# A two-layer hybrid block on one core: longer latencies in the scheduler's table, and RWKV row sums as single fp32 products

## The chip, the cores and the metric

The kernel runs on one core of a Trainium2 chip. The metric is the device time of one execution in microseconds, measured three times; a separate execution was taken with the hardware profiler, and all rows below come from that one. The engines are called PE (TensorE matmul), PEld (its weight loads), DVE (VectorE), ACT (ScalarE), POOL (GpSimd) and SP (the queue that issues DMAs).

## What is computed

Two layers over a sequence of 1024 tokens of width 1024, all in float32. Each layer normalises and modulates its input, projects it into the inputs of three branches, and adds the gated output projection of the three results. The branches are a chunk-causal latent attention (MLA), a chunked state-space branch (SSD) and an RWKV-7 branch. Cut to what matters here:

```python
h = rms_norm(x, norm_w[l]) * (1.0 + scale) + shift
(q_lat, kv_lat, k_pe, g_mla, z, xbc, dt_raw, r, k, v, w_lo, a_lo, g_rwkv) = split_cols(h @ w_in[l], IN_SPLIT_SIZES)
...
y = jnp.concatenate([y_mla, y_ssd, y_rwkv], axis=-1)
x = x + gate * (y @ w_out[l])
```

The RWKV branch has two sums over the 64 channels of a head, one for the norm of `kk` and one for the bonus term:

```python
kk = kk / jnp.maximum(jnp.sqrt(jnp.sum(kk * kk, axis=-1, keepdims=True)), 1e-12)
...
y = y + jnp.sum(r * k * r_k.astype(f32), axis=-1, keepdims=True) * v
```

## The kernel before

Channels lie on the 128 partitions and tokens along the free axis, in halves of 512 tokens. There are four rounds, one for each layer and half. A round has a dense part (`dense`): the output projection of the round two before it (`outproj`, from the third round on), the norm and modulation (`make_h`, which writes eight pairs of `h` tiles), and the input projection of 37 tiles (`inproj`), whose results go to DRAM. Then come the round's consumers (`consumers`): `rwkv`, which handles two heads at a time in four passes p, then `ssd`, then the attention (`mla_latent`, `mla_proj`, `mla`). The last two output projections end the program.

A large float32 product is computed as three products of rounded parts: each operand is split into a high part (F32R, an ACT copy) and a low part (a DVE subtraction), and high by high, high by low and low by high are summed. `split_w` does this for the weights (tiles `wr`, `wh`, `wl`), `make_h` and `y_split` for the other operand (`h`). The small products are plain fp32; the trace has two PE records for each of these, and one for an F32R product or a transpose.

What each engine does in which order is decided ahead of time by a list scheduler in the kernel itself (class `Plan`). All operations are recorded, and `order` plays them through: each engine takes, among the operations whose inputs it expects to be there, the one of highest rank. RWKV has a slightly higher rank than SSD and attention; the products of the dense part have rank 0 and fill what is left; loads, splits and evacuations rank highest. When an input is there follows from a price for each operation (`cost`, `shape`) and from `LATENCY`, a table of nanoseconds between the end of an operation and the start of one that needs it: the first letter is the engine that made it, the second the engine that waits (S is ScalarE, V VectorE, P TensorE, G GpSimd, D a DMA). The order so found is fixed in the program; on the chip each engine follows it and waits where an input is late. Every operation is issued by one line, L396, so all rows carry that line, and groups are told apart by tile names.

The two row sums are in `rwkv_a1` and `rwkv_a2`. With `PQ` and `PB` at 1 the summed tile (`rt`) is split into `leafh` and `leafl`, two tiles of the pool for attention and SSD, and two F32R products against `bones_r` (a block matrix of ones, rounded once at the start) are added in PSUM. In `rwkv_a1` only 2 columns of that matrix are used, so the result has 2 partitions; in `rwkv_a2` all 128 are used. With `PQ` and `PB` at 0 each is one fp32 product against `bones`. There are 4 passes in 4 rounds, so 16 of each kind. The result of the first is copied by ACT, sent through DRAM (`qd`) and read by `tinv_a`, which starts a chain of 62 small DVE operations; that of the second is multiplied by `v` and kept for the end of the pass. The scheduler's `shape` prices an fp32 product with at most 64 columns of weights at 103 ns, whatever its width, and one with more at 1.73 ns a column.

Of the kernel before, what the change touches and what calls it, by code (L numbers as in the profile page):

```python
# [10 lines left out]
F32R = mybir.dt.float32r  # L11
I32 = mybir.dt.int32
AF = mybir.ActivationFunctionType
# [4 lines left out]
P = 128  # L18
# [37 lines left out]
SG = ()  # L56
# [14 lines left out]
SX, SV, SB = 0, 0, 0  # L71
SG0 = "bbgggggg"
SBP, SBC, SCH = "ra", "ra", 2
SRB = "tf"
PQ = 1
PB = 1
PX = "b2"
WAT = "rv"
LOT = "rl"
# [7 lines left out]

LATENCY = {"SS": 143, "SD": 147, "SV": 142, "SP": 500, "SG": 170, "VS": 128, "VD": 122, "VV": 127, "VP": 500, "VG": 155,  # L90
           "PS": 197, "PV": 196, "PD": 220, "PG": 224, "PP": 3, "GS": 75, "GD": 67, "GV": 60, "GP": 135, "GG": 102,
           "DS": 2200, "DV": 2200, "DP": 2350, "DG": 2200, "DD": 2200}


# [149 lines left out]
class Plan:  # L244
# [41 lines left out]
    def order(self):  # L286
# [12 lines left out]
        def seat(o):  # L299
            t = 0.0  # L300
            for name in o.tiles:
                x = tiles[name]
                if x["free"] is None:
                    tag = x["tag"]
                    n = len(slots[tag]) - (0 if name.startswith("leafl") else owed[tag])
                    if n <= name.startswith("leafh") or not name.startswith("leaf") and name not in line[tag][:n]:
                        parked[tag].append(o)
                        return None
                    t = max([t] + [end + LATENCY[at + o.at] for at, (end, _) in slots[tag][0][1].items()])
                else:  # L310
                    t = max([t] + [end + LATENCY[at + o.at] for at, (end, _) in x["free"].items()])
                if x["bank"]:
                    t = max([t] + [end + LATENCY[at + o.at] for at, (end, _) in x["ends"].items() if at != o.at])
            return t
# [10 lines left out]
        while turn < len(ops):  # L325
# [58 lines left out]
            for j in o.next:  # L384
                ready[j] = max(ready[j], end + LATENCY[o.at + ops[j].at])
                wait[j] -= 1
# [11 lines left out]
def hybrid_layers_kernel(ctx: ExitStack, tc: tile.TileContext, A, out):  # L398
    nc = tc.nc
    plan = Plan(tc)  # L400
    V, S, G, PE, SP = (plan.engine(e, q) for e, q in ((nc.vector, "V"), (nc.scalar, "S"), (nc.gpsimd, "G"),
                                                      (nc.tensor, "P"), (nc.sync, "Q")))
    TQ, AL, AS, BL, BM, BS, EQ = SP, S, S, S, SP, S, SP

    cpool = ctx.enter_context(tc.tile_pool(name="cpool", bufs=1))
# [46 lines left out]
    def s1(n, tag=None, bufs=None):  # L452
        if bufs:
            return sm.tile([P, n], F32, name=nm("s"), tag=tag or f"s{n}", bufs=bufs)
        return sm.tile([P, n], F32, name=nm("s"), tag=tag or f"s{n}")

    def bank(tag):
        return ps.tile([P, HT], F32, name=nm("ps"), tag=tag, bufs=PSB[tag])
# [22 lines left out]
    bones = cst[:, C_BO:C_BO + 128]  # L481
# [17 lines left out]
    for e in range(2):  # L499
        SP.dma_start(cst[64:128, C_MD + 64 * e:C_MD + 64 * e + 64], A["cst"][64:128, C_MD + 64 * (1 - e):C_MD + 64 * (1 - e) + 64])  # L500
    SP.dma_start(mD1[64:128], A["cst"][64:128, C_MD:C_MD + 128])
    bones_r = cpool.tile([P, 128], F32R, name="bones_r")
    S.activation(bones_r, bones, AF.Copy)
    cth = s1(8)
    S.activation(cth, craw, AF.Tanh, scale=0.5)
    V.scalar_tensor_tensor(cth, cth, 1.0, craw, op0=ALU.add, op1=ALU.mult)
# [248 lines left out]
    def rwkv_a1(d, U, p, wa):  # L755
# [32 lines left out]
        pq = bank("ra")  # L788
        if PQ:
            hi, lo = WATS[PX](dt=F32R, leaf="leafh"), WATS[PX](dt=F32R, leaf="leafl")  # L790
# [13 lines left out]
    def rwkv_a2(d, p, u):  # L804
# [29 lines left out]
        pbn = bank("ra")  # L834
        if PB:
            hi, lo = WATS[PX](dt=F32R, leaf="leafh"), WATS[PX](dt=F32R, leaf="leafl")
# [917 lines left out]
```

## Time and profile before

| | |
|---|---|
| median of 3 runs (lowest to highest) | 1953.89 us (1953.27 to 1957.49) |
| the profiled execution | 1953.58 us |
| its span, first to last instruction | 1951.8 us |
| busy in the span: PE, DVE, ACT, POOL | 1825.9, 1619.7, 1205.9, 204.4 us |
| mean granted PE clock | 0.975 |

"Busy" is the time that at least one instruction of the engine ran. The page's second part cuts the span into 40 slices of 48.8 us. A matmul record includes the time until its result has left the array, so the pace of a stream is read from the starts of successive records, not from their lengths.

### The profile page before, as it was taken

The numbers are of one execution on the slowest core, as the hardware profiler recorded it, in microseconds if no ns is written. First come the engines' busy times: TensorE is split into PE (matmuls) and PEld (weight loads), VectorE is DVE, ScalarE is ACT, GpSimd is POOL, SyncE is SP. The second block draws the span as 40 slices with busy tenths as digits, with TensorE's granted clock in tenths as the row PEclk, the third lists the DMA queues.
The fourth block names the chain that finished last, engine by engine and source line by source line (L and its number), as shares of the span: only waits on it lengthen the run. The fifth ranks groups of instructions, "written<-read, shape, count | busy, mean of one in ns | idle before, by whom it ended". The sixth has DMA issues, their size and how long they took to land. (4 is left out here: it accounts for less than half of the span.)

```text
span 1951.8 us, 32300 instructions
## 1 busy us (share of the span) xinstructions
PE 1825.9 (94%) x10220; PEld 1460.7 (75%) x10220; DVE 1619.7 (83%) x4002; ACT 1205.9 (62%) x2520; POOL 204.4 (10%) x302
## 2 busy tenths in 40 slices
PE   5899997999999986989999999998999999999996
PEld 3677775888887764777778778787777877888884
DVE  7898898789897999787788978888788896978774
ACT  5566566676665655566657567675656557675652
POOL 2120011011010101020100001002010020001001
PEclk9999998999999986999999999999999999999997
DMA  7677666765658673744464665854456565753542
GB/s 248 219 201 200 182 198 190 225 200 164 190 152 212 195 205 102 238 132 114 122 165 133 157 203 171 272 170 141 131 146 177 157 203 171 246 162 100 183 144 73
DMA packets 273371, 341.31 MB, mean 175 GB/s; under 512 B 79152, under 2 KB 132016, under 8 KB 273200
## 3 DMA queue, kind: packets, MB, share of 16 engines
q1 hardware_dynamic: 273200, 339.25, 59.6%
q8 instruction: 81, 1.33, 0.3%
q14 instruction: 90, 0.74, 0.1%
HBM read 254.67 MB, written 84.47 MB: 174 GB/s over the span
## 5 line engine op out<-in xcount | busy, mean ns | idle before, releaser
L396 PE MATMUL ps<-h,wh 128*128 128x512 f32 x3136 | 1015.9, 407 | 35.3 <-ACT h L396 21.4
L396 PEld LDWEIGHTS ps<-h,wh 128*128 128x128 f32 x3136 | 581.2, 191 | 166.3 <-ACT h L396 26.8
L396 PE MATMUL ps<-h,wl 128*128 128x512 f32 x1568 | 590.1, 407 | 0.1
L396 PE MATMUL ps<-b,b 128*128 128x512 f32 (+4 forms) x1512 | 384.6, 356 | 10.5 <-DVE b L396 6.3
L396 ACT ACTIVATE wh<-wr 128x512 fp32r<-128x512 f32 (+1 forms) x398 | 246.4, 620 | 211.4 <-PE ps L396 164.3
L396 PEld LDWEIGHTS ps<-h,wl 128*128 128x128 f32 x1568 | 296.8, 191 | 56.7 <-issue 2.5
L396 DVE TENSOR_TENSOR wl<-wr,wh 128x512 fp32r<-128x512 f32 (+1 forms) x398 | 269.7, 680 | 59.4 <-ACT wh L396 41.1
L396 PEld LDWEIGHTS ps<-b,b 128*128 128x128 f32 (+1 forms) x1512 | 232.1, 184 | 67.6 <-DVE b L396 14.5
L396 ACT ACTIVATE b<-b 128x512 f32<-128x512 f32 (+3 forms) x222 | 136.9, 625 | 62.1 <-DVE b L396 25.6
L396 ACT ACTIVATE b<-ps 128x512 f32<-128x512 f32 (+3 forms) x201 | 99.4, 508 | 77.8 <-PE ps L396 73.6
L396 DVE TENSOR_TENSOR b<-b,b 128x512 fp32r<-128x512 f32 (+4 forms) x178 | 121.9, 690 | 18.4 <-ACT b L396 14.5
L396 DVE TENSOR_TENSOR rq<-rq,tmp 128x60 f32<-128x60 f32 (+24 forms) x496 | 109.1, 220 | 6.6
L396 DVE TENSOR_TENSOR tmp<-Q,rq 128x60 f32<-128x60 f32 (+24 forms) x496 | 104.3, 210 | 5.9
L396 ACT ACTIVATE ct<-ps 128x512 f32<-128x512 f32 x150 | 87.8, 588 | 24.1 <-PE ps L396 11.2
L396 PE MATMUL ps<-cst,b 128*128 128x128 f32 x452 | 81.6, 282 | 20.7 <-POOL b L396 15.0
L396 PEld LDWEIGHTS ps<-bx,gg 128*128 128x128 f32 x512 | 76.8, 194 | 32.2 <-DVE bx L396 15.8
L396 POOL COPY halo<-ct 128x3 f32<-128x3 f32 x84 | 28.6, 340 | 621.9 <-ACT ct L396 594.2
L396 PE MATMUL ps<-bx,gg 128*128 128x64 f32 x512 | 80.7, 273 | 9.2 <-DVE bx L396 7.6
L396 PEld LDWEIGHTS ps<-cst,b 128*128 128x128 f32 x452 | 58.4, 146 | 35.1 <-POOL b L396 15.0
L396 POOL TENSOR_TENSOR s<-s,nhalf 128x4 f32<-128x4 f32 (+1 forms) x34 | 54.0, 1591 | 258.1 <-DVE s L396 250.5
L396 DVE SCALAR_TENSOR_TENSOR h<-ps,md,h 128x512 f32<-128x512 f32 x72 | 53.5, 746 | 33.2 <-PE ps L396 32.7
L396 ACT ACTIVATE b<-ps,s,s 128x512 f32<-128x512 f32 (+2 forms) x96 | 63.9, 667 | 27.3 <-DVE s L396 24.3
(196 smaller groups left out, 2612.0 us busy)
## 6 DMA issues: line engine op xcount, KB each, us to landing
wr<-in_w_in_dram SPq DMA_DIRECT2D x282, 256.0 KB
U<-ct SPq DMA_DIRECT2D x84, 257.5 KB
wr<-in_w_out_dram SPq DMA_DIRECT2D x80, 256.0 KB
U<-ct SPq DMA_DIRECT2D x64, 256.0 KB
ct<-in_ada_dram SPq DMA_DIRECT2D x64, 256.0 KB
ri<-U SPq DMA_DIRECT2D x52, 257.5 KB
b<-accd SPq DMA_DIRECT2D x96, 128.0 KB
ct<-yd SPq DMA_DIRECT2D x48, 256.0 KB
```

Of the source, the lines that this page charges most:

```text
L396: o.fn(*o.args, **o.kw)
```

## The change

Two things. First, four entries of the table are raised: ScalarE to VectorE from 142 to 300 ns, VectorE to ScalarE from 128 to 280, TensorE to either from 196 or 197 to 350. The table is used by the scheduler alone; no instruction is altered by it, but their order is. Second, the row sums become single fp32 products, and `bones_r` goes.

```diff
-PQ = 1
-PB = 1
+PQ = 0
+PB = 0
...
-LATENCY = {"SS": 143, "SD": 147, "SV": 142, "SP": 500, "SG": 170, "VS": 128, "VD": 122, "VV": 127, "VP": 500, "VG": 155,
-           "PS": 197, "PV": 196, "PD": 220, ...
+LATENCY = {"SS": 143, "SD": 147, "SV": 300, "SP": 500, "SG": 170, "VS": 280, "VD": 122, "VV": 127, "VP": 500, "VG": 155,
+           "PS": 350, "PV": 350, "PD": 220, ...
...
-    bones_r = cpool.tile([P, 128], F32R, name="bones_r")
-    S.activation(bones_r, bones, AF.Copy)
```

What this does to the order is shown at three places. Tile names carry a number that is shifted between the two programs, so the same tile has two numbers.

**Place A**, PE, where the input projection of the first round ends and that of the second begins. `ps_1246` (before) and `ps_1229` (after) spread the norm of the second half over the partitions; `make_h` needs them, and the products on `h_1247` (before) and `h_1230` (after) need `make_h`. Before:

```order
L396 MATMUL ps_574<-h_261,wh_579 128x512
L396 MATMUL ps_574<-h_260,wl_580 128x512
L396 MATMUL ps_1246<-cst,s_381 128x128 x4
L396 MATMUL ps_1263<-h_1247,wh_1265 128x512
L396 MATMUL ps_1263<-h_1248,wh_1265 128x512
L396 MATMUL ps_1263<-h_1247,wl_1266 128x512
L396 MATMUL ps_1263<-h_1249,wh_1265 128x512
L396 MATMUL ps_1263<-h_1250,wh_1265 128x512
```

After:

```order
L396 MATMUL ps_1229<-cst,s_380 128x128 x4
L396 MATMUL ps_573<-h_235,wh_578 128x512
L396 MATMUL ps_573<-h_234,wl_579 128x512
L396 MATMUL ps_573<-h_247,wh_578 128x512
L396 MATMUL ps_1013<-b_1009,b_953 128x512
L396 MATMUL ps_573<-h_248,wh_578 128x512
L396 MATMUL ps_1013<-b_1010,b_953 128x512
L396 MATMUL ps_1031<-b_1023,b_1020 128x128
L396 MATMUL ps_1013<-b_1009,b_954 128x512
L396 MATMUL ps_1036<-b_1023,b_1020 128x256
L396 MATMUL ps_573<-h_247,wl_579 128x512
L396 MATMUL ps_573<-h_259,wh_578 128x512
```

The products that need `make_h` followed at once; now sixteen others stand between, of the first round's last tile (`ps_573`) and of its attention (`ps_1013`, `ps_1031`, `ps_1036`, `ps_1015`). The three groups of transposes of `mla_latent`, which stood among the `h` products behind this place (`ps_969`, `ps_975`, `ps_976`), stand 227 to 272 PE instructions ahead of it now (`ps_952`, `ps_958`, `ps_959`).

**Place B**, PE, in the output projection that opens the third round. `ps_1817` and `ps_1818` (before), `ps_1788` and `ps_1789` (after) are the steps of the RWKV state chain (`chain`) of the second pass of the second round: each step needs what ACT and DVE made of the one before it. `ps_2022`, `ps_2028` and `ps_2029` belong to `mla_latent` of the same round. Before:

```order
L396 MATMUL ps_1815<-bx_1726,Ez_102 128x128 x4
L396 MATMUL ps_2022<-cst,b_2019 128x128 x4
L396 MATMUL ps_1817<-bx_1787,gg_1725 128x64 x5
L396 MATMUL ps_2028<-cst,b_2026 128x128 x4
L396 MATMUL ps_1817<-bx_1787,gg_1725 128x64 x3
L396 MATMUL ps_2029<-cst,s_2027 128x128 x4
L396 MATMUL ps_1818<-bx_1787,gg_1725 128x64 x2
L396 MATMUL ps_2419<-h_2356,wh_2416 128x512
L396 MATMUL ps_2419<-h_2357,wh_2416 128x512
L396 MATMUL ps_2419<-h_2356,wl_2417 128x512
L396 MATMUL ps_2419<-h_2359,wh_2416 128x512
L396 MATMUL ps_2419<-h_2360,wh_2416 128x512
```

After:

```order
L396 MATMUL ps_2421<-h_2393,wh_2419 128x512
L396 MATMUL ps_1788<-bx_1760,gg_1702 128x64 x2
L396 MATMUL ps_2421<-h_2392,wl_2420 128x512
L396 MATMUL ps_2421<-h_2395,wh_2419 128x512
L396 MATMUL ps_2421<-h_2396,wh_2419 128x512
L396 MATMUL ps_2421<-h_2395,wl_2420 128x512
L396 MATMUL ps_2426<-h_2389,wh_2424 128x512
L396 MATMUL ps_1788<-bx_1760,gg_1702 128x64
L396 MATMUL ps_2421<-h_2398,wh_2419 128x512
L396 MATMUL ps_2426<-h_2390,wh_2424 128x512
L396 MATMUL ps_2421<-h_2399,wh_2419 128x512
L396 MATMUL ps_2426<-h_2389,wl_2425 128x512
```

Before, ten products of the chain and twelve transposes stand with nothing between them; now five to twelve output or attention products stand between every one or two of the chain's, and the transposes of `mla_latent` stand 328 to 375 instructions ahead.

**Place B**, DVE: a piece between two of the weight splits (`wl`) of the same output projection. `tmp` and `rq` are the small operations of `tinv_a`; `b_1975`, `b_1976` and `b_1983` belong to `ssd`. Before:

```order
L396 TENSOR_TENSOR wl_2376<-wr_2374,wh_2375 128x512
L396 TENSOR_TENSOR rq_1741<-rq_1741,tmp_1742 128x10x6
L396 TENSOR_TENSOR b_1975<-b_1973,s_1972 128x512
L396 TENSOR_TENSOR tmp_1742<-Q_1737,rq_1741 128x54
L396 TENSOR_TENSOR b_1976<-b_1974,s_1972 128x512
L396 TENSOR_TENSOR rq_1741<-rq_1741,tmp_1742 128x9x6
L396 TENSOR_TENSOR b_1983<-Sg_117,cd_1924 128x256
L396 TENSOR_TENSOR tmp_1742<-Q_1737,rq_1741 128x48
L396 SCALAR_TENSOR_TENSOR ac_1547<-ct_1607,cact,ac_1547 128x512
L396 TENSOR_TENSOR wl_2383<-wr_2381,wh_2382 128x512
```

After, up to the next split:

```order
L396 TENSOR_TENSOR wl_2343<-wr_2341,wh_2342 128x512
L396 TENSOR_TENSOR rq_1716<-rq_1716,tmp_1717 128x18x4
L396 TENSOR_SCALAR bx_1699<-ps_1728,s_1652 64x64
L396 TENSOR_TENSOR tmp_1717<-Q_1712,rq_1716 128x68
L396 SCALAR_TENSOR_TENSOR b_1992<-b_1992,pp_110,ps_1996 128x512
L396 TENSOR_TENSOR rq_1716<-rq_1716,tmp_1717 128x17x4
L396 TENSOR_TENSOR tmp_1717<-Q_1712,rq_1716 128x64
L396 SCALAR_TENSOR_TENSOR gg_1763<-rt_1741,dp_111,rt_1748 64x8x64
L396 TENSOR_TENSOR rq_1716<-rq_1716,tmp_1717 128x16x4
L396 TENSOR_TENSOR gg_1763<-rt_1739,rt_1748 64x8x64
L396 TENSOR_TENSOR tmp_1717<-Q_1712,rq_1716 128x75
L396 TENSOR_REDUCE s_1729<-bm_1726 128x8
```

The work of `ssd` has left the piece. From the split of the first output weight tile of this round to that of the eleventh (`wl_2369` to `wl_2448` before, `wl_2336` to `wl_2415` after) DVE has 179 instructions before and 118 after; 29 of `ssd`, 13 of the rope table and 9 of the norm and gate of `ssd` have left it. In the stretch of ten input weight tiles ahead of it there were 92 and are 102; in the two stretches behind it (to `wl_2510` and `wl_2577` before, `wl_2477` and `wl_2544` after) there were 139 and 177 and are 135 and 217.

## Rows read from the trace of the kernel before

**Rows 1.** The page: the span, part 1 (busy time, share of the span, instructions of each engine), and of part 2 the busy tenths of PE and the granted clock in tenths, in 40 slices.

```profile
span 1951.8 us, 32300 instructions
...
PE 1825.9 (94%) x10220; PEld 1460.7 (75%) x10220; DVE 1619.7 (83%) x4002; ACT 1205.9 (62%) x2520; POOL 204.4 (10%) x302
...
PE   5899997999999986989999999998999999999996
...
PEclk9999998999999986999999999999999999999997
```

**Rows 2.** Busy time by stretch: from and to in us, length, then busy us and instructions of PE, PEld, DVE, ACT, POOL, the granted clock, the DMA share and GB/s.

```profile
570.00:675.00 105.00, 103.14 (x607) 83.32 (x607) 90.26 (x239) 66.71 (x147) 7.48 (x13) 0.98 0.74 192
...
725.00:775.00 50.00, 30.33 (x119) 21.28 (x117) 45.61 (x119) 29.03 (x51) 6.44 (x5) 0.72 0.36 112
...
675.00:800.00 125.00, 92.19 (x489) 69.31 (x488) 114.52 (x270) 71.88 (x136) 10.74 (x11) 0.84 0.56 165
...
300.00:325.00 25.00, 15.45 (x61) 11.22 (x60) 23.77 (x53) 15.26 (x25) 1.22 (x2) 0.85 0.63 201
325.00:345.00 20.00, 18.74 (x82) 14.80 (x81) 16.12 (x31) 10.64 (x18) 5.17 (x7) 0.94 0.64 175
...
884.00:1340.00 456.00, 450.81 (x2589) 363.11 (x2588) 374.81 (x947) 296.79 (x631) 36.55 (x61) 1.00 0.57 166
```

**Rows 3.** PE's timeline at place A: start, length, what ran, and in brackets how long PE was idle before it and what ended that.

```profile
308.26 0.60 PE L396 MATMUL ps<-cst,s 128*128 128x128 f32 x4
312.28 0.50 PE L396 MATMUL ps<-h,wh 128*128 128x512 f32 x1 [3.42 <-ACT h L396]
...
318.80 0.50 PE L396 MATMUL ps<-h,wh 128*128 128x512 f32 x1 [1.02 <-DVE h L396]
...
323.30 1.11 PE L396 MATMUL ps<-cst,b 128*128 128x128 f32 x4 [3.31 <-DVE b L396]
...
332.00 0.65 PE L396 MATMUL ps<-cst,s 128*128 128x128 f32 x4 [0.80 <-POOL s L396]
```

**Rows 4.** PE's timeline at place B; `ps<-bx,gg` are the steps of the chain, two records each.

```profile
735.12 0.66 PE L396 MATMUL ps<-bx,gg 128*128 128x64 f32 x4
...
738.78 1.12 PE L396 MATMUL ps<-bx,gg 128*128 128x64 f32 x4 [2.16 <-DVE bx L396]
740.14 1.08 PE L396 MATMUL ps<-cst,b 128*128 128x128 f32 x4 [0.25 <-DVE rq L396]
...
743.84 0.69 PE L396 MATMUL ps<-bx,gg 128*128 128x64 f32 x2 [1.82 <-DVE bx L396]
747.20 1.12 PE L396 MATMUL ps<-cst,s 128*128 128x128 f32 x4 [2.67 <-POOL s L396]
```

**Rows 5.** Groups of instructions by form: count, busy us, mean ns of one, then idle time of the engine before them.

```profile
L396 DVE TENSOR_TENSOR leafl<-rt,leafh 128x512 fp32r<-128x512 f32 x32 | 22.0, 687 | 2.5 <-ACT leafh L396 2.1
...
L396 ACT ACTIVATE leafh<-rt 128x512 fp32r<-128x512 f32 x32 | 20.0, 626 | 3.0 <-DVE rt L396 2.6
```

**Rows 6.** Timeline of the first row sum with its split, all engines (the product with 2 columns of weights, amid dense products).

```profile
109.76 0.63 ACT L396 ACTIVATE leafh<-rt 128x512 fp32r<-128x512 f32 x1
...
110.62 0.39 PE L396 MATMUL ps<-leafh,bones_r 128*2 128x512 f32 x1
...
110.63 0.68 DVE L396 TENSOR_TENSOR leafl<-rt,leafh 128x512 fp32r<-128x512 f32 x1
110.85 0.62 PE L396 MATMUL ps<-h,wh 128*128 128x512 f32 x2
...
111.77 0.40 PE L396 MATMUL ps<-leafl,bones_r 128*2 128x512 f32 x1
...
112.01 0.63 PE L396 MATMUL ps<-h,wh 128*128 128x512 f32 x2
```

**Rows 7.** PE's timeline in the attention of the last round: each `ps<-b,b` row of two records is one fp32 product 256 wide.

```profile
1905.34 0.59 PE L396 MATMUL ps<-b,b 128*128 128x256 f32 x2
1905.77 0.27 PE L396 MATMUL ps<-cst,b 128*128 128x128 f32 x1
1905.88 0.60 PE L396 MATMUL ps<-b,b 128*128 128x256 f32 x2
1906.31 0.49 PE L396 MATMUL ps<-cst,b 128*128 128x128 f32 x3
```

**Rows 8.** Groups of DVE instructions between 675 and 800 us, columns as in Rows 5.

```profile
L396 DVE TENSOR_TENSOR b<-b,b 128x512 f32<-128x512 f32 (+3 forms) x24 | 16.4, 683 | 1.5 <-ACT b L396 1.4
L396 DVE TENSOR_TENSOR rq<-rq,tmp 128x48 f32<-128x48 f32 (+24 forms) x39 | 8.6, 220 | 0.1
...
L396 DVE SCALAR_TENSOR_TENSOR b<-b,b 128x512 f32<-128x512 f32 x12 | 7.9, 683 | 0.0
```

More of the change, by code (lines that the diff above doesn't have):

```diff
@@ L86 @@
 HALO = set(range(T_WA, T_G)) | set(range(T_XBC, T_XBC + 8))
-LATENCY = {"SS": 143, "SD": 147, "SV": 142, "SP": 500, "SG": 170, "VS": 128, "VD": 122, "VV": 127, "VP": 500, "VG": 155,
-           "PS": 197, "PV": 196, "PD": 220, "PG": 224, "PP": 3, "GS": 75, "GD": 67, "GV": 60, "GP": 135, "GG": 102,
+LATENCY = {"SS": 143, "SD": 147, "SV": 300, "SP": 500, "SG": 170, "VS": 280, "VD": 122, "VV": 127, "VP": 500, "VG": 155,
+           "PS": 350, "PV": 350, "PD": 220, "PG": 224, "PP": 3, "GS": 75, "GD": 67, "GV": 60, "GP": 135, "GG": 102,
            "DS": 2200, "DV": 2200, "DP": 2350, "DG": 2200, "DD": 2200}
```

## The prediction

> **What bounds the kernel now.** I read the page's first two parts, then the busy time by stretch, then PE's timeline where PE is idle. PE is busy 94% of the span and DVE 83% [rows 1]. Over most of it PE sets the pace: from 884 to 1340 us it is busy 450.81 of 456 us, while DVE has 18% to spare [rows 2]. An instruction more on PE there is paid in full, one less on DVE or ACT gives nothing. PE loses time at a few places: the start, the end, and two in between, where the slices of PE and of its granted clock dip together [rows 1]. Place A is 300 to 345 us, where the second round's `make_h` begins. PE is busy 15.45 of 25 and 18.74 of 20 us there, so it idles 10.8 us, at granted clocks of 0.85 and 0.94 [rows 2]. The waits are for ACT or DVE to finish `h`, and for the transposes of `mla_latent`, with nothing else queued ahead of them [rows 3]. Place B is 675 to 800 us. PE is busy 92.19 of 125 us at a mean clock of 0.84, and in its middle 30.33 of 50 at 0.72 (a mixture of the two levels, 1.0 for 2.4 GHz and 0.5 for 1.2 GHz, after PE has begun to idle); DVE is busy 114.52 of 125, that is 92% [rows 2]. PE's waits there are short chain products, each waiting for the DVE work that follows the one before it, back to back [rows 4]. So at B DVE is the bound, and PE waits in order behind it.
>
> The profiled execution took 1953.58 us, of which 1951.8 are the span; the median of the three runs is 1953.89, or 0.3 above. I sum from 1953.6.
>
> **The change, part by part.** *The row sums.* Gone are 32 ACT copies of 626 ns and 32 DVE subtractions of 687 ns, 20.0 and 22.0 us in all [rows 5]. On PE each pair of F32R products becomes one fp32 product. The pair's pace: from the first product to its follower 0.23 us (110.62 to 110.85), from the second to its follower 0.24 (111.77 to 112.01), together 0.47 [rows 6]. No fp32 product 512 wide stands in the trace. The nearest is 256 wide: 0.43 us from its start to that of the transpose behind it, twice over (1905.34 to 1905.77, 1905.88 to 1906.31) [rows 7], hence 0.86 us for 512 columns. The product with 2 columns of weights streams the same 512 columns, and its F32R form takes no less than the full one's 0.23, so I price both alike. That is 0.39 us more for each, 32 x 0.39 = **+12.5 us** on PE. The bounds are 0, if one fp32 product took no longer than the pair, and +12.5; only the 256-wide row is an fp32 product, so I take the upper end. Amid dense products nothing does; at place B, where PE waits for DVE, a few of the 32 cost nothing. The removed copies and subtractions lie beside PE work except at B, and count there. On each sum's own path the copy and the subtraction vanish and 0.4 us comes in: the first sum's result reaches `qd` about 1 us earlier, which no row shows PE waiting for. `bones_r` was one copy at the start, nothing on the path.
>
> The Trainium skill (TensorE: Matmul & The Clock Gate, section Back-to-back issue gap) says that a sustained stream of products 512 wide runs at about 131 ns for each. By that the removed pair would be 0.26 us, and the change would add an estimated 0.60 a time, 19 us in all instead of 12.5. The trace shows 0.23 for one of these in a dense stream, so the measurement decides.
>
> *The table.* It costs no instruction; it moves them. The order shows two effects at the places where PE idled.
>
> Place A: sixteen products, about 16 x 0.23 = 3.7 us at the pace of [rows 6], now stand between the transposes that spread the norm and the first product that needs `make_h`, where there were none and PE waited 3.42 us. The `mla_latent` transposes, which PE waited for 3.31 and 0.80 us [rows 3], are over before the place begins. What stays is that `make_h` itself is a DVE and ACT loop, so the waits of the 1.02 kind remain in part. Of the 10.8 us idle I count **-8 us**; the bounds are 0 and -10.8 plus what the clock gives back, up to 0.15 x 25 = 4 us.
>
> Place B: DVE has 179 instructions in the ten-tile stretch before and 118 after. DVE's mean there is 114.52 / 270 = 0.42 us [rows 2]. So 61 fewer are 26 us less DVE work while the same dense products pass. The two following stretches get -4 and +40, that is 36 x 0.42 = 15 us back. If every one of these lay on the path, the net is -11 us; if none did, -26. Most of those that left are full tiles of 0.68 us (`ssd`, the rope table, the gates), while many of those that came are the 0.22 us operations of `tinv_a` [rows 8]; that puts it nearer the larger end: **-20 us**. The stretch ahead of B takes ten instructions more; DVE was busy 90.26 of 105 us there [rows 2], so it has 14.7 us free, and 10 x 0.42 = 4 us fit. On PE the chain's products at B now have five to twelve others between them, 1.2 us and more, against waits of 1.82 to 2.67 us [rows 4]: so much of each wait is covered. Next in line after DVE is PE itself.
>
> The sum: 1953.6 + 12.5 - 8 - 20 = **1938 us**. Elsewhere the new order moves thousands of instructions by a little; from 884 us on PE waits so rarely that there is little to win, and I put nothing for it but a margin of 10 us either way.
>
> **The rivals.** *The holes close fully.* If DVE's load at B comes down to what PE needs, B's loss goes altogether: 125 us hold 489 PE records, which at the pace of 884 to 1340 (2589 in 456) take 86 us, so 39 us are lost there. With 10.8 at A: 1953.6 + 12.5 - 39 - 11 = 1916. For it: DVE's instructions at B fall by a third. Against it: the stretch behind B gets 40 more.
>
> *The hole moves and the product is paid (slower).* One mechanism: the DVE work taken from B lands where DVE has no room. It has 14.7 us free in the 105 us ahead of B. If the state-space work arrives there later than the order supposes, because its own inputs come from the input projection's last tiles, DVE runs into B with the same 26 us as before, and PE waits at other products. It decides once more than 14.7 us of that work is late. Then only +12.5 remains: 1966, or 1958 if A's gain is kept. For it: total DVE work falls only by 22.0 us [rows 5]. Against it: the chain's products have fill between them, which they lacked.
>
> *The order matters little and the gains cancel the product:* 1953, if B gives 12 us and A none. This is also the case that the table's change does not do on the chip what the order suggests.
>
> *The small row sum is cheap.* The scheduler prices the product with 2 columns of weights at 103 ns. If PE did that, sixteen would cost 0.37 us less than the old pair instead of 0.39 more: 1938 - 12 = 1926. The F32R form with 2 columns shows no such discount [rows 6], so 1 in 20, within the range.
>
> **How the numbers follow.** Forecast near 1938: 0.50 (1926 to 1949). Holes close fully, 1910 to 1926: 0.20, the cheap sum included. Gains cancel the product, within 0.2% (1949.7 to 1957.5): 0.12. The hole moves, 1957.5 to 1970: 0.18. A difference under 0.2%, about 4 us, can't be told from none here. So faster 0.70, same 0.12, slower 0.18. The range leaves out a tenth at either end: 1913 to 1962.
>
> **What would show it.** Right: the granted clock between 675 and 800 us rises from 0.84 to over 0.93, PE's idle time there falls from 33 us to under 15, DVE's share there falls from 92%; at A no wait before `ps<-cst,b`; the 32 products appear as 64 records with 0.43 us between starts. Wrong: a new dip of clock and PE busy ahead of 675 us or behind 850, with DVE over 92% in it; the row sums' pace at 0.23 a record or lower; or a gain that comes from stretches where PE was already full.

## The result, and the profile after

The changed kernel takes 1933.11 us (median of 4 executions, 1930.92 to 1936.69) against 1954.22 for the kernel before on the same chip: a ratio of 0.9894, 95% interval 0.9872 to 0.9916. That is 21 us less, where 16 were forecast (1938 from 1953.9). The time came out as predicted; a good part of the reasons did not, as the experiments show.

The page after, the lines that answer to [rows 1]:

```profile
span 1932.2 us, 32249 instructions
...
PE 1825.1 (94%) x10220; PEld 1451.2 (75%) x10220; DVE 1591.6 (82%) x3970; ACT 1194.1 (62%) x2487; POOL 215.6 (11%) x302
...
PE   5899999999999979979998999998999999999996
...
PEclk9999999999999989989999999999999999999998
```

Of the two slices of place B (the fifteenth and sixteenth, 8 and 6 before) one is full now, the other reads 7; the eighteenth, 821 to 869 us, has fallen from 8 to 7. The clock no longer dips at the seventh slice, where A was. Busy time by stretch after, columns as in [rows 2]:

```profile
300.00:325.00 25.00, 25.00 (x118) 20.34 (x117) 16.27 (x36) 14.31 (x28) 1.61 (x4) 1.00 0.85 261
325.00:345.00 20.00, 19.12 (x120) 13.77 (x120) 17.91 (x30) 13.72 (x26) 1.80 (x3) 1.00 0.93 300
675.00:800.00 125.00, 111.28 (x574) 85.43 (x573) 109.27 (x261) 74.37 (x142) 11.87 (x13) 0.93 0.67 208
800.00:900.00 100.00, 87.39 (x511) 69.36 (x510) 80.05 (x229) 60.92 (x135) 14.89 (x19) 0.91 0.36 106
884.00:1340.00 456.00, 448.85 (x2588) 364.73 (x2587) 371.38 (x963) 292.43 (x615) 51.26 (x71) 1.00 0.58 171
```

To add idle time and a lowered clock into one number I take **lost** = length minus (PE busy times granted clock): an estimate of what a stretch would be shorter by if PE had run at full clock throughout. The clock is the mean of the whole stretch, idle time included, so the estimate is high where PE idles while its clock is low. Added up piece by piece between the steps of the granted clock, 670 to 800 us lose 46.6 us before and 19.7 after, where the estimate says 48.4 and 22.0; in the other kernels of the table below it is up to 5.5 us too high there. The kernel before, in wider stretches that hold a hole wherever an order puts it:

```profile
290.00:370.00 80.00, 68.50 (x387) 53.65 (x385) 66.24 (x134) 49.47 (x91) 9.71 (x17) 0.94 0.70 207
670.00:800.00 130.00, 97.19 (x522) 73.77 (x521) 119.52 (x284) 75.58 (x144) 12.04 (x12) 0.84 0.58 170
800.00:900.00 100.00, 94.19 (x535) 76.99 (x534) 82.95 (x207) 59.01 (x125) 13.62 (x17) 0.95 0.53 164
```

Lost there before: 15.6, 48.4 and 10.5 us. After: 3.0 (77.00 busy of 80 at 1.00), 22.0 (116.13 of 130 at 0.93) and 20.5. So A gave 12.6 and B 26.4, and 10.0 were given back behind B. Most of the signs that the prediction named are there: from 675 to 800 us PE idles 13.7 us for 33, DVE is busy 87% for 92, and the clock is 0.93 for 0.84, just at the bound that it had set. PE's idle time at place B (670 to 800 us), by the products that it stood in front of, shows what closed; behind the second bar stand the idle us and what ended them. Before:

```profile
L396 PE MATMUL ps<-h,wh 128*128 128x512 f32 x102 | 38.2, 451 | 9.6 <-ACT h L396 6.3 <-DVE h L396 2.5 <-ACT ct L396 0.7
...
L396 PE MATMUL ps<-bx,gg 128*128 128x64 f32 x32 | 7.4, 349 | 7.9 <-DVE bx L396 7.5 <-ACT bx L396 0.4
L396 PE MATMUL ps<-gg,bk 128*128 128x128 f32 x40 | 6.4, 312 | 5.3 <-DVE bk L396 3.5 <-ACT bx L396 1.7
...
L396 PE MATMUL ps<-cst,s 128*128 128x128 f32 x8 | 1.8, 360 | 3.3 <-POOL s L396 3.3
```

After:

```profile
L396 PE MATMUL ps<-h,wh 128*128 128x512 f32 x176 | 59.2, 409 | 2.4 <-DVE h L396 1.4 <-ACT ct L396 0.9
...
L396 PE MATMUL ps<-bx,gg 128*128 128x64 f32 x48 | 7.3, 267 | 0.2
...
L396 PE MATMUL ps<-rt,cst 128*2 128x512 f32 (+1 forms) x4 | 3.0, 834 | 6.7 <-ACT rt L396 6.7
```

The waits of the RWKV chain are gone (7.9 to 0.2), those for the `h` tiles have shrunk, and half of the 13.9 us that PE still idles there stands in front of one row sum.

The row sums, PE's timeline after; each row of two records is one product:

```profile
644.74 1.02 PE L396 MATMUL ps<-rt,cst 128*128 128x512 f32 x2
645.61 1.05 PE L396 MATMUL ps<-gt,Tz 128*128 128x128 f32 x8
...
1017.95 1.02 PE L396 MATMUL ps<-rt,cst 128*2 128x512 f32 x2
1018.90 0.50 PE L396 MATMUL ps<-h,wl 128*128 128x512 f32 x1
```

From the start of a product to that of its follower it is 0.87 us with 128 columns of weights and 0.95 with 2. The medians of all that PE doesn't wait behind are 0.43 + 0.43 and 0.43 + 0.52 for the two records. Two new waits are the largest after, behind the one at the start (a third, 4.96 us at 1059.98, is for a DMA):

```profile
688.37 1.87 PE L396 MATMUL ps<-rt,cst 128*2 128x512 f32 x2 [6.65 <-ACT rt L396]
690.17 1.65 PE L396 MATMUL ps<-b,b 128*128 128x512 f32 x3
...
828.95 0.90 PE L396 MATMUL ps<-b,b 128*128 128x128 f32 x3 [5.53 <-ACT b L396]
```

The first is a row sum whose square ACT makes late; the products behind it then follow without a wait of their own. The Trainium skill (TensorE: Matmul & The Clock Gate, section Step-by-step: what each phase is for) says that matmuls stay in program order; these rows agree.

### The profile page after: what moved, and what is told of

The parts are those of the page before. It is cut to its first block, busy times and chain, and to the rows that moved or that the text cites. A ratio compares the mean times of both kernels' runs of the same rounds, so it can differ in the third digit from the quotient of the medians.

```text
span 1932.2 us, 32249 instructions
## 1 busy us (share of the span) xinstructions
PE 1825.1 (94%) x10220; PEld 1451.2 (75%) x10220; DVE 1591.6 (82%) x3970; ACT 1194.1 (62%) x2487; POOL 215.6 (11%) x302
## 4 chain that ended last, share of the span: by engine, by line
PE 72%; DVE 13%; ACT 6%; DMA 5%; issue 3%; POOL 1%; SPq 1%; DVEq 0%; POOLq 0%; ACTq 0%
PE ps L396 72%; DVE h L396 3%; DVE bx L396 2%; DVE wl L396 2%; ACT b L396 2%; DVE s L396 1%; DVE gg L396 1%; DVE rq L396 1%; DVE tmp L396 1%; DVE b L396 1%; ACT wh L396 1%; DMA b<-accd 1%; ACT ct L396 1%; DMA U<-ct 1%; SPq L396 1%
## 5 line engine op out<-in xcount | busy, mean ns | idle before, releaser
L396 PE MATMUL ps<-b,b 128*128 128x512 f32 (+4 forms) x1512 | 379.0, 356 | 18.9 <-ACT b L396 10.9
L396 PEld LDWEIGHTS ps<-b,b 128*128 128x128 f32 (+1 forms) x1512 | 228.8, 182 | 76.2 <-ACT b L396 18.7
L396 DVE TENSOR_TENSOR b<-b,b 128x512 fp32r<-128x512 f32 (+4 forms) x178 | 119.6, 679 | 29.4 <-ACT b L396 19.9
L396 POOL COPY halo<-ct 128x3 f32<-128x3 f32 x84 | 39.4, 469 | 626.0 <-ACT ct L396 625.8
L396 PEld LDWEIGHTS ps<-bx,gg 128*128 128x128 f32 x512 | 79.2, 190 | 18.7 <-DVE bx L396 4.9
L396 ACT ACTIVATE b<-ps,s,s 128x512 f32<-128x512 f32 (+2 forms) x96 | 64.0, 668 | 30.9 <-DVE s L396 29.4
L396 PEld LDWEIGHTS ps<-cst,b 128*128 128x128 f32 x452 | 58.1, 145 | 32.8 <-POOL b L396 14.4
L396 PEld LDWEIGHTS ps<-gg,bk 128*128 128x128 f32 x512 | 66.1, 191 | 9.1 <-issue 2.3
```

Source lines behind the costliest of these rows:

```text
L396: o.fn(*o.args, **o.kw)
```

## The experiments

One table first; the runs and their edits follow it. Each ratio is to the kernel before, run again on the same chip, where its median was 1949 to 1954 us. "Row sums" says whether they are split pairs or single products, "table" whether it is the old or a long one. "In `make_h`" is what PE lost between the first and the last operation of the second round's `make_h` (each kernel's own 12.6 to 18.7 us), and "other work" the PE work within that time that doesn't need its result (the products there, at the paces of [rows 6] and of the rows above). "Latent" is where the last transposes of the second round's `mla_latent` stand in PE's order, in instructions behind (+) or ahead (-) of the third round's first output product. "Lost 290-370" is the wider stretch that holds place A in every one of these orders. "DVE" is the number of DVE instructions in the ten-tile stretch at B, of which the prediction spoke.

| kernel | row sums, table | ratio to before | lost in `make_h` | other work | lost 290-370 | lost 670-800 | latent | DVE | lost 800-900 |
|---|---|---|---|---|---|---|---|---|---|
| before | split, old | 1 | 8.5 | 0.3 | 15.6 | 48.4 | +199 | 179 | 10.5 |
| e10_old_near | split, old + 10 | 1.0136 | 6.9 | 0.0 | 10.6 | 44.2 | +178 | 137 | 14.3 |
| g2_latent_rank | split, old | 1.0066 | 7.4 | 0.0 | 13.0 | 47.5 | +365 | 85 | 26.7 |
| g1_leaf_ct | split, old | 1.0134 | 1.6 | 10.8 | 1.8 | 18.4 | -116 | 138 | 23.6 |
| e1_table | split, long | 1.0165 | 10.3 | 0.2 | 17.7 | 31.3 | +64 | 126 | 20.3 |
| e9_table_near | split, long + 10 | 1.0036 | 2.3 | 4.8 | 3.4 | 52.1 | +354 | 117 | 11.0 |
| e2_sums | single, old | 1.0017 | 9.9 | 1.6 | 15.1 | 30.2 | -44 | 151 | 6.8 |
| e11_sums_near | single, old + 10 | 0.9998 | 1.4 | 10.0 | 19.4 | 24.6 | -1 | 141 | 20.3 |
| after | single, long | 0.9894 | 0.9 | 3.9 | 3.0 | 22.0 | -39 | 118 | 20.5 |
| e6_near | single, long + 10 | 0.9915 | 1.5 | 4.4 | 4.2 | 18.3 | -39 | 124 | 18.9 |
| g3_third_table | single, another long | 0.9855 | 1.6 | 6.4 | 18.2 | 24.9 | -1 | 129 | 6.6 |
| h1_chosen | one of the two single, another long | 0.9839 | 2.5 | 5.6 | 3.6 | 19.9 | -60 | 123 | 28.9 |

The expectations below count A and B along PE's own work: their "550 to 700 us" of place B is the stretch in which PE goes from 550 to 700 us of work done, some 600 to 800 us of the span. The measured losses are those of the table.

**The table alone** (`PQ` and `PB` back at 1, `bones_r` back):

```diff
-PQ = 0
-PB = 0
+PQ = 1
+PB = 1
```

> The new table alone, the row sums left as split pairs. Two separate effects: the single products cost 14 us on PE (32 records pairs at the spacing of the trace after, 29 us, in place of 15), and the table is worth about 35, so this kernel should take 1954 - 35 = 1919 us (1912 to 1926) and beat the changed one; DVE's ten-tile stretch at place B has 126 instructions in it against 179 and 118. Rival, the row sums free DVE at place B: the 22 us of subtractions are what closes the holes there, then the table alone gives 1954 - 5 to 1954 - 10, that is 1944 to 1949. Rival, chance of the order: any other order lands anywhere between 1925 and 1965, with holes at new places.

Measured: 1981.06 us, ratio 1.0165 (1.015 to 1.018), 31 us slower than before. All three expectations missed, mine by 55 us from its upper end. Its `make_h`, and B:

```profile
320.10:332.70 12.60, 3.33 (x10) 2.35 (x9) 12.60 (x23) 9.51 (x15) 0.18 (x1) 0.70 0.36 95
...
670.00:800.00 130.00, 112.13 (x579) 88.86 (x578) 114.53 (x250) 76.79 (x143) 13.74 (x11) 0.88 0.72 220
```

B is less of a hole than before, A is as open as it was, and behind B twice as much is lost (20.3 for 10.5). That does not make 31 us. The largest part of them is lost where the prediction had put nothing, from 1800 us to the end, before and here:

```profile
1800.00:1951.80 151.80, 132.99 (x711) 107.36 (x709) 97.84 (x201) 75.81 (x160) 13.98 (x11) 0.93 0.43 134
```

```profile
1800.00:1978.10 178.10, 143.57 (x737) 113.76 (x736) 99.69 (x223) 80.74 (x177) 9.09 (x7) 0.90 0.35 109
```

These are 28.1 and 48.9 us lost. So places A and B are not all that an order of this table changes. That the table gives 28 us and the products cost 12.5, as the prediction added them up, is not how the change works.

**The single products alone** (the old four entries back; here and below the changed entries alone are shown).

```diff
-"SV": 300, "VS": 280, "PS": 350, "PV": 350
+"SV": 142, "VS": 128, "PS": 197, "PV": 196
```

> The single products alone, the old table. Two separate effects: 1954 + 14 = 1968 us (1961 to 1972), or a few us less where the products stand in PE's waits at place B; the holes at A and B stay, since DVE's ten-tile stretch at B still has 151 instructions. Rival, the row sums free DVE at B: 1954 + 14 - 22 - A's share, 1935 to 1946, with the granted clock of 675 to 800 us above 0.90. Rival, chance of the order: anywhere between 1925 and 1965.

Measured: 1953.27 us, ratio 1.0017 (1.0004 to 1.0031), 3 us slower. Between the first two ranges, so neither; the third, a chance of the order, allows it: PE's extra 14 us are there, but the new order took 18 us off B (30.2 lost).

**The product's price in a fixed order.** A product was marked when it was recorded, and issued twice:

```diff
-                o.fn(*o.args, **o.kw)
+                for _ in range(1 + getattr(o, "twice", False)):
+                    o.fn(*o.args, **o.kw)
```

> The changed kernel in the very same order, with each of the 32 row-sum products issued twice in a row (the second overwrites the first with the same values). If PE pays for a single fp32 product in full, 16 x 0.86 + 16 x 0.95 = 29 us more: 1933 + 29 = 1962 us (1957 to 1965). If part of them lies in time in which PE waits anyway, 1945 to 1955. If they are as good as free (the product is hidden), 1933 to 1937.

Measured: 1954.42 us, ratio 1.0024 (1.0011 to 1.0037), that is 0.0130 above the changed kernel's ratio, or 25 us. A doubled product with 2 columns in its timeline, four records in 1.81 us:

```profile
108.68 1.88 PE L397 MATMUL ps<-rt,cst 128*2 128x512 f32 x4 [0.60 <-ACT rt L397]
110.49 0.50 PE L397 MATMUL ps<-h,wh 128*128 128x512 f32 x1
```

That is 0.43 for each record but the last, whose 0.52 is paid once, where PE goes on to another product. So the doubling adds 32 x 0.86 = 27.5 us of PE time, 1.5 less than I had expected, and 25 of them reach the end (20 to 30 by the two intervals): PE pays for the product in full or nearly so. The expectation had set 1957 us or more for this case, counted from 1933; where this was run the kernel before takes 1950 us and not 1954, so the ratio decides.

**The order of before with the work of after.** The split was recorded, so that the order stayed, and left out at issue; one fp32 product took the place of the second of the pair.

```diff
+                if hasattr(o, "instead"):
+                    if o.instead:
+                        o.fn(*o.instead)
+                    continue
                 o.fn(*o.args, **o.kw)
```

> The kernel before in its own order, word for word, but each pair of row-sum products is issued as one fp32 product at the place of the pair's second, and the 32 copies and 32 subtractions are left out. This parts the work from the order. If PE pays for the product and nothing else changes: +14 us against the kernel before, less what falls into PE's waits (about +10 to +14). If the 32 subtractions taken from DVE matter, they can do so only where DVE bounds, and 3 of them stand between 675 and 800 us and 1 between 300 and 345: 2.8 us back at most, +10 or a little less. If the single products themselves are worth what two edits together gave, 15 to 20 us less than before.

Measured: 1957.49 us, ratio 1.0039 (1.002 to 1.0057): +8 us, between 4 and 11. So in one and the same order the second half of the change costs 8 us, a little under what was expected: 14 us for the products, less what lies in waits and what the freed ACT and DVE give, which this run does not part. B stays as it was:

```profile
670.00:800.00 130.00, 100.00 (x525) 75.15 (x525) 117.94 (x279) 73.55 (x140) 11.63 (x12) 0.84 0.54 172
```

That is 46.0 lost for 48.4. The work taken from DVE and ACT does next to nothing for B; what the single products did in e2_sums they did through the order.

**Is it a chance of the order?** Four kernels whose four entries are 10 ns higher than those of the changed kernel, of the table alone, of the kernel before and of the single products alone. For the first:

```diff
-"SV": 300, "VS": 280, "PS": 350, "PV": 350
+"SV": 310, "VS": 290, "PS": 360, "PV": 360
```

> The changed kernel with the four raised entries 10 ns higher still (310, 290, 360, 360), which puts nearly all operations at another place in the order. If the longer table is the cause by what it stands for (room between a producer and a consumer), 10 ns more change little: 1933 within 8 us (1925 to 1941), with PE's idle total near the 97 us of the changed kernel. If the gain is a chance of this one order, the time lands elsewhere: more than 12 us off, up to 1965, with holes at other places.

Measured: 1933.80 us, ratio 0.9915 (0.9898 to 0.9932), the same as the changed kernel within the intervals.

> The table alone (row sums split), with the four entries 10 ns higher still. The table alone took 1981. If that loss belongs to the long table with split row sums, this one loses too: 1970 to 1990. If it is the chance of one order, this draw is independent of it: anywhere between 1920 and 1975, with PE's holes at other places; DVE's ten-tile stretch at place B has 117 instructions here against 126, and the one behind it 216 against 111.

Measured: 1957.56 us, ratio 1.0036 (1.0021 to 1.0051), 25 us below e1_table. A is closed here, B lost 52.1 us.

For the third:

```diff
-"SV": 142, "VS": 128, "PS": 197, "PV": 196
+"SV": 152, "VS": 138, "PS": 207, "PV": 206
```

> The kernel before (row sums split) with the four old entries 10 ns higher (152, 138, 207, 206), no other edit. DVE's ten-tile stretch at place B has 137 instructions in this order against 179 before. If the 179 were what made the hole at B, and the old order had drawn them by chance, 10 ns are enough to lose them: 42 x 0.42 us less DVE work there, up to 18 us faster than before (1930 to 1942). If the length of the table is what counts, 10 ns of 158 do nothing: 1945 to 1955, and the hole at B stays.

Measured: 1977.27 us, ratio 1.0136 (1.0109 to 1.0162): 27 us slower than before by 10 ns in four prices. The stretch at B has 137 DVE instructions for 179, and B loses 44.2 us for 48.4; the time is lost elsewhere (among others 34.7 us from 1800 us to the end, for 28.1). At B:

```profile
670.00:800.00 130.00, 103.38 (x530) 77.69 (x528) 111.64 (x253) 73.96 (x141) 12.48 (x13) 0.83 0.59 183
```

> The single products with the four old entries 10 ns higher. The single products with the old table took 3 us more than before. If the orders of one table are alike, 1953 within 5 us. If each order is a draw of its own, anywhere from 1930 to 1970. PE's work is the same as in the changed kernel, so what differs is its idle time and the granted clock alone.

Measured: 1948.68 us, ratio 0.9998 (0.998 to 1.0016), within 5 us of e2_sums. So with split sums the time is a draw over some 30 us (1.0000 to 1.0165 in four orders of the scheduler's own); with single ones two draws of either table agree within 5 us, and the long table is 0.8 to 1.2% ahead of the old one in both. Two draws of each are few. Within its `make_h` this order loses 1.4 us only, but the hole has not closed, it stands ahead of `make_h` (15.1 us lost from 290 to 315 us):

```profile
290.00:315.00 25.00, 16.76 (x56) 12.08 (x55) 21.68 (x52) 10.71 (x22) 3.92 (x6) 0.59 0.38 116
670.00:800.00 130.00, 114.60 (x591) 88.81 (x591) 116.80 (x272) 79.05 (x147) 14.86 (x14) 0.92 0.69 218
```

**What opens B.** The split tiles come from the pool that attention and SSD share, and the single products need none. Two kernels move `mla_latent` in opposite ways, with table and split sums of before. In the first the split takes its tiles elsewhere, in the second `mla_latent` gets a higher rank.

```diff
-PX = "b2"
+PX = "ct"
```

> The kernel before with its old table and its split row sums; only the two tiles of each split are taken from another pool (`ct`, that of the evacuations) and no longer from the 17 tiles that attention and SSD share. In its order the transposes of `mla_latent` end 438 PE instructions ahead of the second round's first input product and 116 ahead of the third round's first output product, where they ended 46 and 199 behind them. Theory of the late attention: what opens the holes is that attention's opening chain runs into `make_h`, because the split tiles keep SSD and attention waiting for room. Then both holes close with nothing of the table changed: place A (14 us lost before) to under 5, the 550 to 700 us of place B (49 us lost) to under 30, in all 1950 - 10 - 20 = 1920 us, plus what the evacuations lose by sharing their four tiles, which I can't price: 1915 to 1945. Theory of the prediction (the longer table closes them): the holes stay, 1950 or more.

Measured: 1975.55 us, ratio 1.0134 (1.011 to 1.0159). The two holes did close, in an order of the old table with split sums; the time missed by 30 us, since as much and more is lost elsewhere:

```profile
348.20:366.90 18.70, 17.09 (x85) 12.80 (x84) 17.63 (x34) 14.30 (x28) 1.00 (x2) 1.00 0.86 249
...
670.00:800.00 130.00, 116.22 (x615) 88.56 (x614) 111.38 (x280) 78.21 (x156) 11.14 (x15) 0.96 0.68 214
...
1330.00:1400.00 70.00, 53.53 (x303) 43.43 (x301) 44.42 (x109) 33.10 (x77) 8.02 (x10) 0.78 0.27 80
```

The last stretch alone loses 28 us here and 9 before (64.47 busy at 0.95). That the shared pool of the evacuations does this was not shown.

```diff
-            mla_latent(d, U, m)
+            with plan.ahead(20000):
+                mla_latent(d, U, m)
```

> The kernel before with one rank raised: `mla_latent` above RWKV, table and row sums as before. In this order its transposes end 129 PE instructions ahead of the second round's first input product (46 behind it before), but 365 behind the third round's first output product (199 before), while DVE's ten-tile stretch at place B holds only 85 instructions (179 before). Theory of the late attention: place A closes (14 us lost to under 6) and place B stays as bad or gets worse (49 us lost to 45 or 65), in all 1940 to 1965. Theory of the prediction (B is the number of DVE instructions in its stretch): B closes, 94 x 0.42 us = 39 us less DVE work there, in all 1910 to 1925.

Measured: 1961.79 us, ratio 1.0066 (1.0044 to 1.0087). B stays open, with half as many DVE instructions in its stretch and DVE busy 107.64 of 130 us:

```profile
314.80:328.50 13.70, 10.08 (x22) 6.39 (x22) 13.64 (x29) 7.07 (x11) 0.37 (x2) 0.63 0.35 123
...
670.00:800.00 130.00, 100.61 (x545) 78.21 (x542) 107.64 (x261) 68.74 (x144) 8.92 (x10) 0.82 0.48 148
```

Its transposes of `mla_latent` run at 805 to 813 us, and waits have gone there with them:

```profile
805.41 1.09 PE L396 MATMUL ps<-cst,b 128*128 128x128 f32 x4 [2.91 <-DVE b L396]
807.28 1.12 PE L396 MATMUL ps<-cst,b 128*128 128x128 f32 x4 [0.79 <-DVE s L396]
811.61 1.11 PE L396 MATMUL ps<-cst,s 128*128 128x128 f32 x4 [3.21 <-POOL s L396]
```

These 6.9 us lie behind the stretch, though, and the 29.4 us that PE idles within it are before other products. The two largest groups, from 670 to 800 us:

```profile
L396 PE MATMUL ps<-h,wh 128*128 128x512 f32 x152 | 51.5, 428 | 5.3 <-ACT h L396 4.6 <-ACT ct L396 0.8
...
L396 PE MATMUL ps<-leafh,bones_r 128*128 128x512 f32 (+1 forms) x2 | 1.0, 490 | 6.2 <-ACT leafh L396 6.2
```

So the position of `mla_latent` foretold rightly that B stays open, but the waits in it are not for its transposes.

At A my own expectation fell: `mla_latent` stood ahead of it, and it stayed open (7.4 lost in `make_h`). What parts the orders there is the other work. Between the ends of `make_h`, before and after:

```profile
310.70:323.80 13.10, 6.17 (x17) 3.77 (x18) 13.08 (x23) 6.70 (x11) 0.26 (x2) 0.75 0.63 215
```

```profile
328.40:341.60 13.20, 12.32 (x49) 8.45 (x48) 13.20 (x23) 8.83 (x16) 1.61 (x2) 1.00 0.93 303
```

`make_h` keeps DVE busy for 13 us in both. The orders that leave PE 3.9 us or more of other work meanwhile lose 0.9 to 2.5 us, those with 1.6 or less 6.9 to 10.3. That holds within `make_h` alone: in e11_sums_near and in g3_third_table, the next run, 14 to 15 us are lost just ahead of it instead, and 290 to 370 us lose more than before.

**Two more tables.**

```diff
-"SV": 300, "VS": 280, "PS": 350, "PV": 350
+"SV": 280, "VS": 370, "PS": 320, "PV": 320
```

> The changed kernel with other long entries: ScalarE to VectorE 280, VectorE to ScalarE 370, TensorE to either 320. PE's work is the same. Its order has the transposes of `mla_latent` ended 181 and 1 PE instructions ahead of the two openings (244 and 39 in the changed kernel), and the scheduler's own end of the program 21 us earlier. Theory of the late attention: the holes at A and B stay small (under 5 and under 30 us) and the time is that of the changed kernel or better, 1915 to 1935. If each order is a draw with nothing to go by: 1925 to 1965.

Measured: 1922.27 us, ratio 0.9855 (0.9834 to 0.9876). Inside `make_h` 1.6 us are lost and at B 24.9, as expected; just ahead of A a hole of another kind opened (16.27 busy of 25 at a clock of 0.66 from 290 to 315 us, 14 lost), and the hole behind B is gone (6.6).

```diff
-PQ = 0
+PQ = 1
...
-"SV": 300, "VS": 280, "PS": 350, "PV": 350
+"SV": 400, "VS": 310, "PS": 370, "PV": 370
```

> An order chosen by two readings, among some sixty orders of other long tables: ScalarE to VectorE 400, VectorE to ScalarE 310, TensorE to either 370, and of the two row sums only the one with 128 columns as a single product (the other stays a pair, 16 x 0.48 = 8 us less on PE than in the changed kernel). First reading: place A closes if the order holds 3.9 us or more of PE work that doesn't need `make_h` between its first and last step; here it is 5.3. Second: place B is small if the transposes of `mla_latent` end ahead of the third round's first output product; here 60 instructions ahead. If both readings hold, A loses under 5 us, 550 to 700 us lose under 30, and the time is 1912 to 1930 us. If the position says nothing and each order is a draw, 1925 to 1965, with A or B open.

Measured: 1917.35 us (the median of five), ratio 0.9839 (0.9818 to 0.9861); one of the five executions took 6171 us, which no run here explains, and is left out of the ratio. Both readings held:

```profile
318.90:332.60 13.70, 11.18 (x49) 8.04 (x48) 13.42 (x24) 12.39 (x24) 0.37 (x2) 1.00 0.88 268
...
670.00:800.00 130.00, 118.38 (x635) 94.51 (x634) 115.04 (x293) 78.09 (x157) 12.62 (x11) 0.93 0.63 201
800.00:900.00 100.00, 82.70 (x469) 67.27 (x468) 75.41 (x200) 56.52 (x127) 14.57 (x18) 0.86 0.30 90
```

It is faster than both kernels, the changed one included (the intervals do not meet), though 28.9 us are still lost behind B. Of the 11 us by which it beats the changed kernel, some 8 are the price that the pair saves on the other row sum.

The two readings are not enough to find a fast order. Six kernels of the table meet both (3.9 us or more of other work, `mla_latent` ahead): after, e6_near, g3_third_table and h1_chosen are 0.9 to 1.6% faster than before, e11_sums_near takes the same time, and g1_leaf_ct is 1.3% slower.

## Why the prediction was right, and where not

**What bounds the kernel.** That PE sets the pace and loses at a few places held: what was gained was gained at A and B. "At B DVE is the bound" did not. In g2_latent_rank DVE has 12 us less to do at B than before (107.64 for 119.52), and PE still idles 29.4 us there for 32.8, at a clock of 0.82 for 0.84; in e11_sums_near DVE is busier than that (116.80) and PE idles 15.4. What PE waits for at B is one late chain after another in its own order; that DVE was 92% busy there was no proof that it was the limit.

**The row sums, +12.5.** Right in kind and nearly in size; the upper end was the right one, and the measured price lies a little above it: 16 x 0.86 and 16 x 0.95 are 29 us, for 15 before, so +14. The product with 2 columns, priced like the full one, costs 0.09 us more; the rival that it is cheap is refuted. By the estimate from the Trainium skill (TensorE: Matmul & The Clock Gate, section Back-to-back issue gap) the change would have added 19 us; the rows decide for 14. In the order of before 4 to 11 us reach the end. Waits were missed: in the changed kernel PE idles 12 us in front of the 32 products, 6.65 of it at 688.37, where ACT makes the square late; in front of the pairs before it was 0.5, and with the old table (e2_sums) it is 0.2, so the waits come with the new order.

**Place A, -8.** The mechanism was the right one, sixteen products (3.7 us) between the spread of the norm and the first product that needs `make_h`; the size was low, 12.6 us. The waits of the 1.02 kind, which I had left standing, went too: PE idles 0.88 us from 300 to 345 us, at clocks of 1.00.

**Place B, -20.** The size was near (26.4), the reason wrong. The step that failed is "61 fewer are 26 us less DVE work while the same dense products pass". From 675 to 800 us DVE's work fell by 5 us (114.52 to 109.27), not by 26, while PE's idle time fell by 19. The other half of the argument, that the chain's products now have others between them, held: 7.9 us of waits became 0.2. Nor does the count go with the loss in other orders: 85 instructions lose 47.5 us, 151 lose 30.2. What goes with it is where `mla_latent` stands. The four orders with its transposes 178 instructions or more behind the output projection's opening lose 44 to 52 us, one at +64 loses 31.3, and the seven with them ahead lose 18 to 30. The prediction saw that move ("stand 328 to 375 instructions ahead" in the text on the change) and did not price it. In these orders it goes together with the row sums (the four have split pairs, all of the seven but g1_leaf_ct single products), but f1_before_order has single products, the transposes where the kernel before has them, and loses 46.0. That the position is the cause is supported from both sides, by a pool (closed) and a rank (still open), but both edits move other work too, and in the second PE's waits at B are not for these transposes. So for B the position is a sign that held in every run; how it acts was not shown.

**Which half did it.** The prediction gave the whole gain to the table and the whole cost to the row sums. Neither half alone gains: the table alone is slower by 31 us in one draw and by 7 in another, the single products alone take 3 us more and none. Since an edit of the work also edits the order, the two do not add. B's part is there with the single products and the old table (30.2 and 24.6 lost); A's, over 290 to 370 us, is there in four of six orders with a long table, and in none of the four that the scheduler draws from the old one as it stands or 10 ns higher (10.6 to 19.4 lost). And A and B do not decide the time alone: e1_table and g1_leaf_ct lose less at B than before and are 31 and 26 us slower.

**The rivals.** *The hole moves*: half of it came true. DVE did not run into B, but a hole of 10 us more stands at 800 to 900 us, where the prediction had set its sign of error, though with DVE at 80% and not over 92%. The largest wait in it is the one of 5.53 us for a `b` tile of ACT. In the twelve kernels of the table that stretch loses 7 to 29 us, with no relation that I found; its cause stays open. *The holes close fully* and *the gains cancel the product* did not come.

**The sum.** +14, -12.6, -26.4 and +10.0 make -15; the span fell by 19.6. The remaining 5 us are spread over the rest, within the margin of 10. That the total came within 5 us of the forecast is in part luck: A and B gave 11 us more than it had counted, and the 10 us lost behind B, which it had priced at nothing, took most of that back.

## What to carry to other kernels

When a list scheduler fixes the order, an edit of its prices or of one operation redraws everything: run the neighbours (the same table 10 ns on) before a difference of 1% is put down to the edit, and hold the order fixed when the price of an operation is wanted. Look at what PE has to do while a serial stage on DVE and ACT runs, and at how far the opening chain of the next consumer stands from it; both can be read from the order. They told here which holes would close, and one order picked by them was the fastest, but two others that met them were no faster than before: holes elsewhere decide too, so the order has to be run. A busy share of 92% beside a waiting PE doesn't say which of the two is the limit; kernels in which that share differs do.

## What was not expected of the hardware

An fp32 product 512 wide with 2 columns of weights takes 0.95 us from start to start and one with 128 columns 0.86: fewer columns save nothing here. The extra 0.09 stands behind the last record alone (0.52 for 0.43); doubled, the product adds only 0.86. The split pair with 2 columns shows none of it (0.23 for each of its records, before). In f1_before_order, with other products around them, the spacings of the single products are the same.
